# Three PSUM tiles in place of one for the spread of the batch-norm parameters

## The chip, the cores and the metric

The kernel runs on one core of a Trainium2 chip. The metric is device time in microseconds (us). All profiles told here were taken in the fast state, with a granted TensorE clock of 1.0. A profile's span (from the first instruction to the last) is 1.7 to 2.0 us shorter than the time of the same execution.

## The reference, cut to what matters

```python
batch, channels, h, w = 32, 128, 32, 32          # x is 16.78 MB of float32
normalized = (x - running_mean) / sqrt(running_var + eps)
out = maximum(normalized * gamma + beta, 0)       # per channel, in inference
```

So out = relu(x * scale + bias), with one scale and one bias for each channel. The chip has to read 16.78 MB and write 16.78 MB and does little else.

## The kernel before

A row of 1024 values belongs to one channel. 16 rows lie on each of 128 partitions, in two halves of 8 MB each (t = 0 and 1). Loads go out on the queue of SP, parameters and stores on that of ACT.

```python
TILES = ((0, 0, 2), (0, 2, 4), (0, 4, 8), (0, 8, 16), (1, 0, 16))
LOAD_CUTS = {(1, 8)}        # the last tile is loaded in two transfers
STORE_CUTS = {(0, 1)}       # the first tile is stored in two
...
raw = params.tile([Q, 4, J], F32, name="raw")
for k, src in enumerate((running_var, gamma, running_mean, beta)):
    nc.scalar.dma_start(out=raw[:, k, :], in_=src.rearrange("(q j) -> q j", j=J))
...
cols = psum.tile([P, 4, J], F32, name="cols")
for a, b in ((0, 2), (2, 3), (3, 4)):             # three matmuls into one PSUM tile
    nc.tensor.matmul(cols[:, a:b, :] ..., rep ..., raw[:, a:b, :] ..., start=True, stop=True)
nc.scalar.activation(out=std_t, in_=cols[:, 0, :], func=ACTF.Sqrt, bias=eps_t[:, 0:1], scale=1.0)
nc.vector.reciprocal(out=rstd_t, in_=std_t)
nc.vector.tensor_mul(out=scale_t, in0=cols[:, 1, :], in1=rstd_t)
nc.vector.tensor_mul(out=ms_t, in0=cols[:, 2, :], in1=scale_t)
nc.vector.tensor_sub(out=bias_t, in0=cols[:, 3, :], in1=ms_t)
# then on ACT, in order: relu(scale * x + bias) row by row in place, and a store after each tile
...
```

Every transfer of x moves one unbroken piece for each of the 128 partitions, eight pieces for each of the 16 DMA engines. The packet records of the trace show one packet for a piece: loads of 8, 8, 16, 32, 32 and 32 KB, stores of 4, 4, 8, 16, 32 and 64 KB. The records give queue, start, duration and size, but not the engine. What is said here of single engines comes from chaining: a packet starts within a few ns of the end of the one before it on its engine. With work on both queues the packets of a chain nearly always alternate, one load and one store, whatever their size (702 of 720 successions in the changed kernel; chains may be crossed where two packets end together). I call one load packet on each of the 16 engines a *load turn*. The 32 KB loads make 24 load turns.

Of the kernel before, what the change touches and what calls it, by code (L numbers as in the profile page):

```python
# [1 line left out]

# [4 lines left out]


F32 = mybir.dt.float32
ACTF = mybir.ActivationFunctionType  # L10



J = 16

TILES = ((0, 0, 2), (0, 2, 4), (0, 4, 8), (0, 8, 16), (1, 0, 16))

LOAD_CUTS = {(1, 8)}
STORE_CUTS = {(0, 1)}

HALVES = {(1, 0), (1, 1)}


@with_exitstack
def kernel(
    ctx: ExitStack,
    tc: tile.TileContext,
    x: bass.AP,
    gamma: bass.AP,
    beta: bass.AP,  # L30
    running_mean: bass.AP,
    running_var: bass.AP,
    eps: bass.AP,
    out: bass.AP,
):
    nc = tc.nc
    B, C, H, W = x.shape
    HW = H * W
    P = nc.NUM_PARTITIONS
    assert C % J == 0 and P % (C // J) == 0 and (B * C) % (P * J) == 0  # L40
    Q = C // J
    T = B * C // (P * J)

    xr = x.rearrange("b c h w -> (b c) (h w)").rearrange("(t p j) w -> t p j w", p=P, j=J)
    outr = out.rearrange("b c h w -> (b c) (h w)").rearrange("(t p j) w -> t p j w", p=P, j=J)

    data = ctx.enter_context(tc.tile_pool(name="data", bufs=1))
    params = ctx.enter_context(tc.tile_pool(name="params", bufs=1))
    psum = ctx.enter_context(tc.tile_pool(name="psum", bufs=1, space=bass.MemoryType.PSUM))

    tiles = []
    for t, a, b in TILES:
        xt = data.tile([P, b - a, HW], F32, name=f"x{t}_{a}")
        cuts = [a] + [j for j in range(a + 1, b) if (t, j) in LOAD_CUTS] + [b]
        for c, d in zip(cuts, cuts[1:]):
            nc.sync.dma_start(out=xt[:, c - a : d - a, :], in_=xr[t, :, c:d, :])  # L56
        tiles.append((t, a, b, xt))



    raw = params.tile([Q, 4, J], F32, name="raw")
    for k, src in enumerate((running_var, gamma, running_mean, beta)):
        nc.scalar.dma_start(out=raw[:, k, :], in_=src.rearrange("(q j) -> q j", j=J))
    eps_t = params.tile([P, 1], F32, name="eps_t")
    nc.vector.memset(eps_t, float(eps))  # L65
    rep = params.tile([Q, P // Q, Q], F32, name="rep")
    nc.gpsimd.memset(rep, 1.0)  # L67
    nc.gpsimd.affine_select(  # L68
        out=rep,
        in_=rep,  # L70
        compare_op=mybir.AluOpType.is_equal,
        fill=0.0,
        base=0,
        pattern=[[0, P // Q], [-1, Q]],
        channel_multiplier=1,
    )
    cols = psum.tile([P, 4, J], F32, name="cols")


    for a, b in ((0, 2), (2, 3), (3, 4)):  # L80
        nc.tensor.matmul(  # L81
            cols[:, a:b, :].rearrange("p k j -> p (k j)"),
            rep.rearrange("q r s -> q (r s)"),
            raw[:, a:b, :].rearrange("q k j -> q (k j)"),
            start=True,
            stop=True,
        )
    std_t = params.tile([P, J], F32, name="std_t")
    nc.scalar.activation(out=std_t, in_=cols[:, 0, :], func=ACTF.Sqrt, bias=eps_t[:, 0:1], scale=1.0)  # L89
    rstd_t = params.tile([P, J], F32, name="rstd_t")  # L90
    nc.vector.reciprocal(out=rstd_t, in_=std_t)  # L91
    scale_t = params.tile([P, J], F32, name="scale_t")
    nc.vector.tensor_mul(out=scale_t, in0=cols[:, 1, :], in1=rstd_t)  # L93
    ms_t = params.tile([P, J], F32, name="ms_t")
    nc.vector.tensor_mul(out=ms_t, in0=cols[:, 2, :], in1=scale_t)  # L95
    bias_t = params.tile([P, J], F32, name="bias_t")
    nc.vector.tensor_sub(out=bias_t, in0=cols[:, 3, :], in1=ms_t)  # L97

    with tc.manual_schedule(engines={mybir.EngineType.Activation}):
        for t, a, b, xt in tiles:  # L100
            first = a
            for j in range(a, b):
                step = HW // 2 if (t, j) in HALVES else HW
                for w in range(0, HW, step):
                    nc.scalar.activation(  # L105
                        out=xt[:, j - a, w : w + step],
                        in_=xt[:, j - a, w : w + step],
                        func=ACTF.Relu,
                        bias=bias_t[:, j : j + 1],
                        scale=scale_t[:, j : j + 1],  # L110
                    )
                if j + 1 == b or (t, j + 1) in STORE_CUTS:
                    nc.scalar.dma_start(
                        out=outr[t, :, first : j + 1, :], in_=xt[:, first - a : j + 1 - a, :]
                    )
                    first = j + 1


# [1 line left out]
_INS = ['x', 'gamma', 'beta', 'running_mean', 'running_var', 'eps']  # L120
_OUTS = [((32, 128, 32, 32), 'float32')]

_NUMBERS = {'eps': 1e-05}


# [26 lines left out]
```

## Time and profile before

| | kernel before |
|---|---|
| time, median of 3 | 83.53 us (83.52 to 83.58) |
| span of the profile | 81.7 us |
| loads (q1), share of 16 engines' span | 48.6%, or 39.7 us |
| stores (q10) | 47.8%, or 39.1 us |
| ACT busy | 39.1 us |
| last x load landed, last store issued | 46.74 us, 55.95 us |

A share in the queue table is the time that the packets of a queue took, over the time of 16 engines. Multiplied by the span it gives microseconds in which all 16 engines work for that queue.

The prediction doesn't show the chain of waits as lines. Here are its two longest pieces before (start, length, what):

```profile
8.11 38.63 DMA x<-in_x_dram
...
47.91 8.01 ACT x L105 x7
```

The last load of x, issued at 8.11, lands 38.63 us later, and the last activations follow.

### The profile page before, as it was taken

The page shows a single profiled execution, that of the slowest core. Times are in us where ns is not written, and L with a number is a line of the kernel's source. Part 1 is how long each engine was busy: PE and PEld are TensorE (multiplying, and loading weights), DVE is VectorE, ACT ScalarE, POOL GpSimd, SP SyncE. Part 2 cuts the span into 40 slices and gives each one's busy share as a digit, 9 for nine tenths or more (in the row PEclk, how much of TensorE's full clock was granted, in tenths as well). Part 3 has the DMA queues.
Part 4 walks back from the last instruction along what each step waited for, and adds up shares of the span by engine and source line. Part 5 has one row for each costly group of instructions (what it writes and reads, how often), then busy time and mean ns, then how long its engine had stood idle before and what let it go on. Part 6 is the DMA issues. An engine that isn't in the chain of part 4 may idle for free.

```text
span 81.7 us, 128 instructions
## 1 busy us (share of the span) xinstructions
PE 1.7 (2%) x6; PEld 1.5 (2%) x6; DVE 0.8 (1%) x5; ACT 39.1 (48%) x36; POOL 0.8 (1%) x6
## 2 busy tenths in 40 slices
PE   0008000000000000000000000000000000000000
PEld 0007000000000000000000000000000000000000
DVE  0000300000000000000000000000000000000000
ACT  0600477799039999199997199993000000000000
POOL 3000000000000000000000000000000000000000
DMA  2899999989899898969789699996991999998290
GB/s 44 313 422 481 409 481 417 497 369 497 369 385 481 375 491 357 541 293 605 321 373 589 273 489 393 513 497 273 513 770 64 449 513 513 513 513 385 128 513 0
DMA packets 1793, 33.56 MB, mean 411 GB/s; under 512 B 257, under 2 KB 257, under 8 KB 513
## 3 DMA queue, kind: packets, MB, share of 16 engines
q1 hardware_dynamic: 864, 16.78, 48.6%
q10 hardware_dynamic: 928, 16.78, 47.8%
q14 instruction: 1, 0.00, 0.0%
HBM read 16.78 MB, written 16.78 MB: 411 GB/s over the span
## 4 chain that ended last, share of the span: by engine, by line
DMA 56%; ACT 10%; issue 2%; SPq 0%
DMA x<-in_x_dram 56%; ACT x L105 10%; SPq L56 0%
## 5 line engine op out<-in xcount | busy, mean ns | idle before, releaser
L105 ACT ACTIVATE x<-x,bias_t,scale_t 128x1024 f32<-128x1024 f32 (+1 forms) x34 | 37.5, 1178 | 10.0 <-DMA x<-in_x_dram 7.7
L89 ACT ACT_TABLE_LOAD x1 | 1.3, 1283 | 2.7 <-issue 2.7
L89 ACT ACTIVATE std_t<-cols,eps_t 128x16 f32<-128x16 f32 x1 | 0.3, 276 | 4.2 <-PE cols L81 4.2
L81 PE MATMUL cols<-raw,rep 8*128 8x16 f32 (+1 forms) x6 | 1.7, 384 | 6.4 <-DMA raw<-in_gamma_dram 6.3
L81 PEld LDWEIGHTS cols<-raw,rep 8*128 8x128 f32 x6 | 1.5, 307 | 6.5 <-issue 6.3
L68 POOL TENSOR_SCALAR_AFFINE_SELECT rep<-rep 8x128 f32<-8x128 f32 x1 | 0.4, 394 | 0.1
L91 DVE RECIPROCAL rstd_t<-std_t 128x16 f32<-128x16 f32 x1 | 0.3, 253 | 7.5 <-ACT std_t L89 7.5
L67 POOL MEMSET rep<- 8x128 f32 x1 | 0.2, 195 | 0.3 <-POOLq L133 0.3
L93 DVE TENSOR_TENSOR scale_t<-cols,rstd_t 128x16 f32<-128x16 f32 x1 | 0.2, 174 | 0.1
L95 DVE TENSOR_TENSOR ms_t<-cols,scale_t 128x16 f32<-128x16 f32 x1 | 0.2, 174 | 0.0
L97 DVE TENSOR_TENSOR bias_t<-cols,ms_t 128x16 f32<-128x16 f32 x1 | 0.2, 174 | 0.0
L133 POOL MEMSET const-bfloat16-1.0<- 128x1 bf16 x1 | 0.1, 108 | 0.0
L133 POOL MEMSET const-float32-0.0<- 128x1 f32 x1 | 0.1, 105 | 0.3 <-issue 0.3
L133 POOL MEMSET const-uint8-127<- 128x1 uint8 x1 | 0.1, 107 | 0.0
L133 POOL MEMSET const-float32-1.0<- 128x1 f32 x1 | 0.1, 105 | 0.0
L65 DVE MEMSET eps_t<- 128x1 f32 x1 | 0.1, 59 | 0.9 <-PEq L133 0.9
## 6 DMA issues: line engine op xcount, KB each, us to landing
x<-in_x_dram SPq DMA_DIRECT2D x3, 4096.0 KB, 38.6
out_dram<-x ACTq DMA_DIRECT2D x1, 4096.0 KB, 28.6
x<-in_x_dram SPq DMA_DIRECT2D x2, 1024.0 KB, 5.8
x<-in_x_dram SPq DMA_DIRECT2D x1, 2048.0 KB, 11.3
out_dram<-x ACTq DMA_DIRECT2D x1, 2048.0 KB
out_dram<-x ACTq DMA_DIRECT2D x2, 512.0 KB, 19.1
out_dram<-x ACTq DMA_DIRECT2D x1, 1024.0 KB
raw<-in_running_var_dram ACTq DMA_DIRECT2D x1, 0.5 KB
```

What stands on the lines that cost most here:

```text
L65: nc.vector.memset(eps_t, float(eps))
L67: nc.gpsimd.memset(rep, 1.0)
L68: nc.gpsimd.affine_select(out=rep, in_=rep, compare_op=mybir.AluOpType.is_equal, fill=0.0, base=0, pattern=[[0, P // Q], [-1, Q]], channel ...
L81: nc.tensor.matmul(cols[:, a:b, :].rearrange("p k j -> p (k j)"), rep.rearrange("q r s -> q (r s)"), raw[:, a:b, :].rearrange("q k j -> q ...
L89: nc.scalar.activation(out=std_t, in_=cols[:, 0, :], func=ACTF.Sqrt, bias=eps_t[:, 0:1], scale=1.0)
L91: nc.vector.reciprocal(out=rstd_t, in_=std_t)
L93: nc.vector.tensor_mul(out=scale_t, in0=cols[:, 1, :], in1=rstd_t)
L95: nc.vector.tensor_mul(out=ms_t, in0=cols[:, 2, :], in1=scale_t)
L97: nc.vector.tensor_sub(out=bias_t, in0=cols[:, 3, :], in1=ms_t)
L105: nc.scalar.activation(out=xt[:, j - a, w : w + step], in_=xt[:, j - a, w : w + step], func=ACTF.Relu, bias=bias_t[:, j : j + 1], scale=sc ...
L133: nc = _bacc.Bacc("TRN2", target_bir_lowering=False, num_devices=1)
```

## The change

The intent: the square root reads only the columns of the first matmul. In one shared tile it waits for all three. With a tile for each matmul it waits for its own, and the activations and stores can start earlier.

```diff
-    raw = params.tile([Q, 4, J], F32, name="raw")
-    for k, src in enumerate((running_var, gamma, running_mean, beta)):
-        nc.scalar.dma_start(out=raw[:, k, :], ...)
+    raw = {}
+    for a, srcs in ((0, (running_var, gamma)), (2, (running_mean,)), (3, (beta,))):
+        raw[a] = params.tile([Q, len(srcs), J], F32, name=f"raw{a}")
+        for k, src in enumerate(srcs):
+            nc.scalar.dma_start(out=raw[a][:, k, :], ...)
...
-    cols = psum.tile([P, 4, J], F32, name="cols")
+    cols = []
     for a, b in ((0, 2), (2, 3), (3, 4)):
+        c = psum.tile([P, b - a, J], F32, name=f"cols{a}")
         nc.tensor.matmul(
-            cols[:, a:b, :]..., rep..., raw[:, a:b, :]...,
+            c..., rep..., raw[a]...,
             start=True, stop=True)
+        cols.append(c)
...   # the square root and the DVE steps read cols[0], cols[1], cols[2]
```

More of the change, by code (lines that the diff above doesn't have):

```diff
@@ L57 @@
         tiles.append((t, a, b, xt))
-    raw = params.tile([Q, 4, J], F32, name="raw")
-    for k, src in enumerate((running_var, gamma, running_mean, beta)):
-        nc.scalar.dma_start(out=raw[:, k, :], in_=src.rearrange("(q j) -> q j", j=J))
+    raw = {}
+    for a, srcs in ((0, (running_var, gamma)), (2, (running_mean,)), (3, (beta,))):
+        raw[a] = params.tile([Q, len(srcs), J], F32, name=f"raw{a}")
+        for k, src in enumerate(srcs):
+            nc.scalar.dma_start(out=raw[a][:, k, :], in_=src.rearrange("(q j) -> q j", j=J))
     eps_t = params.tile([P, 1], F32, name="eps_t")
@@ L76 @@
     )
-    cols = psum.tile([P, 4, J], F32, name="cols")
+    cols = []
     for a, b in ((0, 2), (2, 3), (3, 4)):
+        c = psum.tile([P, b - a, J], F32, name=f"cols{a}")
         nc.tensor.matmul(
-            cols[:, a:b, :].rearrange("p k j -> p (k j)"),
+            c.rearrange("p k j -> p (k j)"),
             rep.rearrange("q r s -> q (r s)"),
-            raw[:, a:b, :].rearrange("q k j -> q (k j)"),
+            raw[a].rearrange("q k j -> q (k j)"),
             start=True,
@@ L87 @@
         )
+        cols.append(c)
     std_t = params.tile([P, J], F32, name="std_t")
-    nc.scalar.activation(out=std_t, in_=cols[:, 0, :], func=ACTF.Sqrt, bias=eps_t[:, 0:1], scale=1.0)
+    nc.scalar.activation(
+        out=std_t, in_=cols[0][:, 0, :], func=ACTF.Sqrt, bias=eps_t[:, 0:1], scale=1.0
+    )
     rstd_t = params.tile([P, J], F32, name="rstd_t")
@@ L92 @@
     scale_t = params.tile([P, J], F32, name="scale_t")
-    nc.vector.tensor_mul(out=scale_t, in0=cols[:, 1, :], in1=rstd_t)
+    nc.vector.tensor_mul(out=scale_t, in0=cols[0][:, 1, :], in1=rstd_t)
     ms_t = params.tile([P, J], F32, name="ms_t")
-    nc.vector.tensor_mul(out=ms_t, in0=cols[:, 2, :], in1=scale_t)
+    nc.vector.tensor_mul(out=ms_t, in0=cols[1][:, 0, :], in1=scale_t)
     bias_t = params.tile([P, J], F32, name="bias_t")
-    nc.vector.tensor_sub(out=bias_t, in0=cols[:, 3, :], in1=ms_t)
+    nc.vector.tensor_sub(out=bias_t, in0=cols[2][:, 0, :], in1=ms_t)
     with tc.manual_schedule(engines={mybir.EngineType.Activation}):
```

## The prediction

> **What bounds the kernel now.** I read four views in this order: the page, the chain of waits, a table of stretches, and the timeline of the start.
>
> The page first, its slices and its DMA queues:
>
> ```profile
> span 81.7 us, 128 instructions
> ...
> ACT  0600477799039999199997199993000000000000
> ...
> DMA  2899999989899898969789699996991999998290
> ...
> q1 hardware_dynamic: 864, 16.78, 48.6%
> q10 hardware_dynamic: 928, 16.78, 47.8%
> ...
> HBM read 16.78 MB, written 16.78 MB: 411 GB/s over the span
> ```
>
> ScalarE (ACT) is done after slice 28 of 40; the DMA engines are busy from the second slice to the last but one. Loads (q1) take 48.6% of the time of 16 engines and stores (q10) 47.8%: 96.4% of 81.7 us, or 78.8 us, in which all 16 are moving bytes. Single slices jump (a packet is counted where its record falls), so I averaged over long stretches. The table of stretches says, with the DMA share in the last column but one:
>
> ```profile
> 2.00:20.00 18.00, 1.75 (x6) 1.49 (x6) 0.78 (x4) 10.80 (x10) 0.00 (x0) 1.00 1.00 419
> 20.00:40.00 20.00, 0.00 (x0) 0.00 (x0) 0.00 (x0) 14.62 (x16) 0.00 (x0) 1.00 1.01 432
> 40.00:60.00 20.00, 0.00 (x0) 0.00 (x0) 0.00 (x0) 13.65 (x12) 0.00 (x0) 1.00 1.03 444
> 60.00:80.00 20.00, 0.00 (x0) 0.00 (x0) 0.00 (x0) 0.00 (x0) 0.00 (x0) 1.00 0.97 421
> ```
>
> From 2 to 80 us the share is 1.00, 1.01, 1.03 and 0.97: there is no hole to fill. That includes the stretch in which the parameters are made. Before 2 us stands the launch and the first load's latency; after 80 us only the last landing and the closing barriers.
>
> The chain of waits of the page (part 4) attributes 56% to the loads of x and 10% to ACT line 105, then stops at the last activation. It leaves out the last store, which is 24.9 us from issue to landing. So the chain is a chain of data, and the load in it is long because the engines share their time with stores; I take the shares of the DMA engines, not this chain, as the bound.
>
> Last, the start, where the change acts:
>
> ```profile
> 6.33 1.78 PE L81 MATMUL cols<-raw,rep 8*128 8x32 f32 x6 [6.33 <-DMA raw<-in_gamma_dram]
> 8.15 0.28 ACT L89 ACTIVATE std_t<-cols,eps_t 128x16 f32<-128x16 f32 x1 [4.21 <-PE cols L81]
> 8.45 0.25 DVE L91 RECIPROCAL rstd_t<-std_t 128x16 f32<-128x16 f32 x1 [7.52 <-ACT std_t L89]
> 8.82 0.17 DVE L93 TENSOR_TENSOR scale_t<-cols,rstd_t 128x16 f32<-128x16 f32 x1
> 9.03 0.17 DVE L95 TENSOR_TENSOR ms_t<-cols,scale_t 128x16 f32<-128x16 f32 x1
> 9.23 0.17 DVE L97 TENSOR_TENSOR bias_t<-cols,ms_t 128x16 f32<-128x16 f32 x1
> 9.44 1.24 ACT L105 ACTIVATE x<-x,bias_t,scale_t 128x1024 f32<-128x1024 f32 x1 [1.02 <-DVE bias_t L97]
> ```
>
> Six TensorE passes (two for each matmul) end at 8.11 and the square root begins at 8.15, straight after the last of them. It needs only the first matmul, whose two passes end at 6.94 (the second starts at 6.54 and takes 0.40). So it waits for two matmuls that it doesn't read.
>
> **What the Trainium skill says.** "DMA: Bandwidth & Descriptors", section "Issuing engines are not separate DMA queues": transfers from SP and ACT run on the same 16 engines and interleave. The trace agrees: q1 and q10 together fill 96.4% of one set of 16. Its "Specifications" give 435 GB/s as the ceiling of the fabric and about 358 GB/s as the HBM limit for a core; the trace has 419 to 444 GB/s in the four stretches, so it is at the first and above the second, and the measurement decides. "PSUM — Partial Sum Buffer", section "PSUM bank collisions raise a hardware error": a TensorE write and a ScalarE or VectorE read of one bank must be kept apart by waits even where the columns differ. That is why one shared tile makes a reader of columns 0 to 15 wait for the writers of columns 32 to 63; with three tiles that wait can go, if they lie in different banks. I have not seen the addresses; the changed kernel builds and passes the race and memory check. "Perfetto Trace Analysis", section "Identifying Dependency Chains": an instruction that waits on several engines may have an extra semaphore instruction before it. The trace agrees: scale_t, the only one of the four DVE steps that waits on two semaphores, starts 0.11 us after the step before it (8.45 + 0.25 to 8.82), the next two only 0.03 after theirs.
>
> **The change part by part.** The comparison of the two instruction orders shows the same instructions on every engine in the same order: four parameter loads, six TensorE passes, one square root, four DVE steps, 34 activations, six stores, six loads of x. No bytes are added and no duration has a reason to change. Only waits move:
>
> 1. *Removed:* the square root's wait for the second and third matmul. It can start at 6.94 + 0.04 = 6.98 in place of 8.15.
> 2. *Unchanged:* the three matmuls wait for the same four parameter loads, and each already waited for its own slice. TensorE starts at 6.33 as before and the third matmul ends at 8.11.
> 3. *Added:* ms_t and bias_t now each wait for a matmul as well as for the DVE step before. From the row of scale_t that costs 0.11 - 0.03 = 0.08 us each.
> 4. *The new short chain:* square root 6.98 to 7.26; reciprocal from 7.28 (same 0.02 distance as now) to 7.53; scale_t 7.64 to 7.81; ms_t 7.92 to 8.09 (second matmul done at 7.48: its second pass starts at 7.11 and takes 0.37); bias_t 8.20 to 8.37, third matmul done at 8.11, so it doesn't bind. The first activation follows at 8.41, where it now starts at 9.44: **1.0 us earlier**. Gain 1.17, less 0.16 for the two added waits.
> 5. *What lies behind it:* the first four activations and three stores move 1.0 us earlier (first store issued about 9.7, now 10.71), and so do the next four (from 15.61 to about 14.6; their 2 MB load lands about 13.0: issued near 1.7, 11.3 to landing). Then ACT reaches a wait that no parameter ends:
>
> ```profile
> 23.84 9.16 ACT L105 ACTIVATE x<-x,bias_t,scale_t 128x1024 f32<-128x1024 f32 x8 [3.59 <-DMA x<-in_x_dram]
> 33.02 0.34 ACTq L113 DMA_DIRECT2D out_dram<-x  x1
> ...
> 46.77 9.16 ACT L105 ACTIVATE x<-x,bias_t,scale_t 128x1024 f32<-128x1024 f32 x8 [2.27 <-DMA x<-in_x_dram]
> 55.95 0.34 ACTq L113 DMA_DIRECT2D out_dram<-x  x1
> ```
>
> The 3.59 us of idle time before 23.84 become about 4.6. The 1.0 us is swallowed there, 24 us into the kernel.
>
> 6. *The sum:* on the DMA engines, 0 packets removed, 0 added, 0 holes closed. The span stays 81.7 and the time 83.5.
>
> **The rivals.**
>
> *A: the 1.0 us comes through.* If the end hung on the chain from the parameters over the activations to the stores, all of it would show: 83.53 - 1.0 = 82.5 us, 1.2%, still under 2%. For it: a store can only start after an activation. Against it: the engines have loads to move in that time, so an earlier store displaces a load, and the last activations wait for loads. I give it 3%.
>
> *B: earlier stores delay the loads and the last store comes too late.* Store packets would take turns with load packets from about 1.0 us sooner. The packet records show a 32 KB load packet at 1.22 us and a 4 KB store packet at 0.16 us, one of each in turn, so 1.0 us is less than one turn (1.38 us): one more store packet of 0.16 to 0.31 us on each engine before the last load lands. Landing 46.74 becomes 46.9 to 47.05, and the issue of the last store 55.95 becomes 56.1 to 56.25. Does that open a hole? The packets of the last store start at 60.90, and those of the store before end at 61.24, without a gap; from the end of its issue (56.29) to its first packet there are 4.6 us. The first store took 3.5 us for the same (11.09 to 14.56), while queued behind loads, so at least 1.1 us of slack remain for a delay of at most 0.3. A hole would cost its own length; at worst a few tenths: 83.8 us. I give it 5%.
>
> *C: the added waits or a late tile eat the gain.* If x's first tile were late, the first activation would not move. It isn't: the first load lands 4.8 us after its issue at 0.81, under 6 us. If the three tiles lay in one bank and waited still, nothing would move at all. Either way the time is 83.5, the same as mine, and only the start of the trace tells it apart.
>
> **Range and chances.** The three runs before lie between 83.52 and 83.58. The engines do 78.8 us of packets plus fixed ends in both kernels; what can differ is how the 16 engines finish (their last packets now end between 80.29 and 80.56, a spread of 0.27) and scatter between chips. So 83.5, with 83.3 to 83.7 to hold it 8 times in 10. Faster by over 2% needs 1.67 us, more than the whole 1.0 us that moves: 1%. Slower by over 2% needs a hole of 1.67 us, against a possible delay of 0.3 and slack of 1.1: 1%. Within 2%: 98%.
>
> **What would show each step right or wrong.** Right: the square root at about 7.0, the first activation at about 8.4, first store issue at about 9.7, idle time before the eight activations near 24 us grown from 3.59 to about 4.6, last store issued between 55.9 and 56.3, DMA share about 1.00 in all four stretches, span 81.6 to 81.8. Step 1 is wrong if the square root still starts after 8.1; step 3 if the gaps before ms_t and bias_t stay at 0.03 or exceed 0.11; step 5 if the eight activations near 24 us move earlier by more than 0.3. The prediction as a whole is wrong if the last store is issued more than 1 us later, if the DMA share falls below 0.95 in a stretch before 80 us, or if packets of the same size take longer than before.

## The result, and the profile after

The changed kernel takes 84.12 us (median of 6, 83.90 to 84.20), the kernel before 83.50 in the same rounds (83.41 to 83.58). The ratio is 1.007, 95% interval 1.0056 to 1.0084. A ratio is the mean time of one kernel's fast runs over that of the other's of the same rounds, so it is not quite the ratio of the medians quoted here. The 0.6 us are clear of the scatter, and 84.12 is outside the range of 83.3 to 83.7. The two traces lie a little further apart than the medians: that of the kernel before is of an execution of 83.44 us, that of the changed kernel of 84.20, the slowest of its six.

The start first, in the timeline of the changed kernel (start, length, engine, line, operation, and in brackets the idle time before it and what ended it):

```profile
6.30 1.76 PE L84 MATMUL cols<-raw,rep 8*128 8x32 f32 x6 [6.30 <-DMA raw<-in_gamma_dram]
6.95 0.27 ACT L93 ACTIVATE std_t<-cols,eps_t 128x16 f32<-128x16 f32 x1 [3.06 <-PE cols L84]
...
7.62 0.17 DVE L99 TENSOR_TENSOR scale_t<-cols,rstd_t 128x16 f32<-128x16 f32 x1
7.89 0.17 DVE L101 TENSOR_TENSOR ms_t<-cols,scale_t 128x16 f32<-128x16 f32 x1
8.17 0.18 DVE L103 TENSOR_TENSOR bias_t<-cols,ms_t 128x16 f32<-128x16 f32 x1
8.39 1.24 ACT L111 ACTIVATE x<-x,bias_t,scale_t 128x1024 f32<-128x1024 f32 x1 [1.17 <-DVE bias_t L103]
```

The intent worked. The square root starts at 6.95 in place of 8.15 and the first activation at 8.39 in place of 9.44.

Later in the same timeline come the points where ACT waits for loads, and the last store:

```profile
24.03 9.16 ACT L111 ACTIVATE x<-x,bias_t,scale_t 128x1024 f32<-128x1024 f32 x8 [4.84 <-DMA x<-in_x_dram]
...
47.85 9.16 ACT L111 ACTIVATE x<-x,bias_t,scale_t 128x1024 f32<-128x1024 f32 x8 [3.19 <-DMA x<-in_x_dram]
57.03 0.34 ACTq L119 DMA_DIRECT2D out_dram<-x  x1
```

At 24 us ACT is already 0.19 us later than before (23.84), and at 47.85 it is 1.08 us later (46.77). The chain of waits gives the reason in one line: the last load takes 39.67 us from issue to landing in place of 38.63.

```profile
8.15 39.67 DMA x<-in_x_dram
```

Now the page, the lines that answer to those of before:

```profile
span 82.5 us, 129 instructions
...
ACT  0601778993039999199996079996000000000000
...
DMA  1999999989898989789789499997991999999190
...
q1 hardware_dynamic: 864, 16.78, 48.8%
q10 hardware_dynamic: 928, 16.78, 47.3%
...
HBM read 16.78 MB, written 16.78 MB: 407 GB/s over the span
```

The queue table is where the loss shows. Loads take 48.8% of 82.5 us, or 40.3 us, in place of 39.7. Stores take 47.3%, or 39.0 us, as before. Packets and bytes are the same. So the same load packets took 0.55 us longer, on the average over the 16 engines, out of a span that grew by 0.8.

The table of stretches has the stretch, its length, the busy time of five engines, the clock, the DMA share and GB/s. For the changed kernel:

```profile
2.00:20.00 18.00, 1.75 (x6) 1.49 (x6) 0.78 (x4) 11.04 (x10) 0.00 (x0) 1.00 1.01 423
20.00:40.00 20.00, 0.00 (x0) 0.00 (x0) 0.00 (x0) 14.22 (x14) 0.00 (x0) 1.00 0.99 424
40.00:60.00 20.00, 0.00 (x0) 0.00 (x0) 0.00 (x0) 13.81 (x13) 0.00 (x0) 1.00 1.02 425
60.00:80.00 20.00, 0.00 (x0) 0.00 (x0) 0.00 (x0) 0.00 (x0) 0.00 (x0) 1.00 1.03 446
```

The share is 1.00 in all stretches here too. It can't tell a slow packet from a fast one: an engine in a slow packet is busy. GB/s can. The stretch 34 to 48 us, in which the last eight load turns run, is first shown for the kernel before, then for the changed one:

```profile
34.00:48.00 14.00, 0.00 (x0) 0.00 (x0) 0.00 (x0) 10.95 (x12) 0.00 (x0) 1.00 1.02 438
```

```profile
34.00:48.00 14.00, 0.00 (x0) 0.00 (x0) 0.00 (x0) 9.87 (x11) 0.00 (x0) 1.00 1.02 415
```

The share is 1.02 in both, but the engines moved 438 GB/s before and 415 after.

The packet records of the trace give the place. All packets of a size take the same time when nothing disturbs them: 309 ns for 8 KB, 611 for 16, 1213 for 32, 2418 for 64. A 4 KB packet takes 159 ns. In both traces no store packet is more than 20 ns above its figure. The 32 KB load packets average 1221 ns before and 1246 after, so 24 of them lose 0.6 us on each engine. Most of that falls in one place: the very last load turn, which starts at 45.0 us in the changed kernel, takes 1.75 to 1.93 us on all 16 engines (mean 1.80). Before, it takes 1.21 to 1.33 (mean 1.245). The first loads of 8 KB are slow in both (0.56 us per engine over 309 ns a packet before, 0.43 after), but the last of them is followed by the first 16 KB packet at the same time in both (7.46 and 7.47 us in the mean), so they don't explain it.

### The profile page after: what moved, and what is told of

It is laid out like the page before. It is cut to its first block, busy times and chain, and to the rows that moved or that the text cites. A ratio compares the mean times of both kernels' runs of the same rounds, so it can differ in the third digit from the quotient of the medians.

```text
span 82.5 us, 129 instructions
## 1 busy us (share of the span) xinstructions
PE 1.7 (2%) x6; PEld 1.5 (2%) x6; DVE 0.8 (1%) x5; ACT 39.1 (47%) x36; POOL 0.8 (1%) x6
## 3 DMA queue, kind: packets, MB, share of 16 engines
q1 hardware_dynamic: 864, 16.78, 48.8%
q10 hardware_dynamic: 928, 16.78, 47.3%
## 4 chain that ended last, share of the span: by engine, by line
DMA 56%; ACT 10%; issue 2%; SPq 0%
DMA x<-in_x_dram 56%; ACT x L111 10%; SPq L56 0%
## 6 DMA issues: line engine op xcount, KB each, us to landing
x<-in_x_dram SPq DMA_DIRECT2D x3, 4096.0 KB, 39.7
```

## The experiments

The theory after the result: **turns**. The first store is issued 1.06 us earlier, so the first store packet of an engine comes after one 32 KB load packet in place of two. In that alignment (the order in which load and store packets stand beside each other) loads are slowed by the stores beside them, most of all the last load turn. Rivals: the tiles themselves cost something (addresses, added waits); the slow packets fall at random; the late loads and the stores beside them clash in memory by their addresses; the load queue runs empty behind the last turn.

This table sums up the traces. "Loads, us" is the q1 share times the span, from each page. The next three columns are counted in the packet records: how many 32 KB load packets an engine has moved before its first store packet, the mean of all 384 such load packets, and the mean of the last 16 of them. A packet or turn that is so many ns *over* took that much longer than an undisturbed packet of its size. Times are medians, but a trace is of one execution: those of the changed kernel (84.20 us) and of a_late_first (83.98) are of their slowest.

| run | first store issued, us | load packets ahead | loads, us | 32 KB load, mean ns | its last turn, mean ns | time, us | ratio |
|---|---|---|---|---|---|---|---|
| before | 10.71 | 2 | 39.7 | 1221 | 1245 | 83.53 | 1 |
| b_again | 10.59 | 2 | 39.8 | 1226 | 1213 | 83.63 | 1.0017 |
| changed | 9.65 | 1 | 40.3 | 1246 | 1803 | 84.12 | 1.0070 |
| a_again | 9.57 | 1 | 40.3 | 1246 | 1588 | 84.14 | 1.0073 |
| p_psum_only | 9.55 | 1 | 40.3 | 1247 | 1629 | 84.17 | 1.0065 |
| a_delay05 | 10.15 | 2, on two engines 1 | 39.8 | 1227 | 1366 | 84.07 | 1.0073 |
| a_delay10 | 10.84 | 2 | 39.8 | 1223 | 1213 | 83.62 | 1.0010 |
| a_late_first | 11.53 | mostly 3 | 40.1 | 1238 | 1311 | 83.72 | 1.0027 |
| a_delay20 | 12.18 | 3 | 40.1 | 1236 | 1519 | 84.02 | 1.0054 |
| a_delay33 | 13.30 | mostly 4 | 40.3 | 1247 | 1612 | 84.27 | 1.0084 |
| b_late_stores | 32.6 | 20 | 40.5 | 1256 | 1791 | 84.37 | 1.0110 |
| a_late_stores | 32.6 | 20 | 40.4 | 1250 | 1911 | 84.29 | 1.0094 |

### Both kernels again

No edit.

> The kernel before, unchanged, for a second trace of it. All theories: ratio 1.000 within 0.002, about 83.5 us. If slow load packets are what costs the changed kernel its time (in its trace the 32 KB load packets took 1246 ns in the mean against 1221 before, with one turn of all 16 engines at about 1.8 us near 45 us), this trace must again show a mean near 1220 ns and no such turn. If slow turns fall at random, this trace may show one too.

> The changed kernel, unchanged, for a second trace of it. Ratio 1.006 to 1.008. Timing theory (earlier stores put load and store packets in another alignment, and loads are slowed by that): slow load packets at the same place again, a turn of about 1.8 us near 45 us on all engines. Chance theory: slow packets elsewhere or none, and then the 0.6 us must be visible somewhere else.

Measured: 83.63 and 84.14 us, ratios 1.0017 (1.0004 to 1.003) and 1.0073 (1.006 to 1.0086). The second trace of the kernel before has no slow last turn (all 16 packets at 1213 ns); the second trace of the changed one has it again, 1588 ns in the mean. So the slow turn isn't chance. The first run also says how far a ratio may stray with the same code: 0.0017. Differences below about 0.003 are not read in what follows.

### One part of the change alone: the PSUM tiles

```diff
 # of the change, only this part; the four parameters stay in one raw tile
-    cols = psum.tile([P, 4, J], F32, name="cols")
+    cols = []   # one PSUM tile for each matmul, appended in the loop
```

> One part of the change alone: three PSUM tiles, but the four parameters stay in one raw tile. The matmuls already waited each for its own part of the raw tile, so the early start must come from the PSUM tiles alone: square root at about 7.0, first store issued at about 9.65, and the whole loss: 1.006 to 1.008. If the raw tiles carried part of the loss, less: 1.000 to 1.004.

Measured: 84.17 us, 1.0065 (1.0037 to 1.0094), the first store issued at 9.55 us. The PSUM tiles carry all of the early start and the loss. The raw tiles do nothing that shows.

### The early start undone, the tiles kept

```diff
-    for a, b in ((0, 2), (2, 3), (3, 4)):
+    for a, b in ((2, 3), (3, 4), (0, 2)):      # a_late_first
```

> Three PSUM tiles and three raw tiles kept, but the matmul that the square root needs is issued last, so that the early start is undone: square root at about 8.1 us, first activation at about 9.4. Timing theory: the loss goes, ratio 0.998 to 1.002. Theory that the tiles themselves cost (addresses, banks, more waits): the loss stays, 1.006 to 1.008.

```diff
+    junk = params.tile([P, 930], F32, name="junk")                     # a_delay10
+    nc.gpsimd.memset(junk, 0.0)
     with tc.manual_schedule(engines={mybir.EngineType.Activation}):
+        nc.scalar.activation(out=junk, in_=junk, func=ACTF.Relu,
+                             bias=bias_t[:, 0:1], scale=scale_t[:, 0:1])
```

> The changed kernel with one activation on a scratch tile of 128x930 ahead of the first activation on x, which takes about 1.05 us of ACT: first activation on x back at about 9.4 us with the whole of the change kept. Timing theory: ratio 0.998 to 1.002. Tile theory: 1.006 to 1.008, and if ACT time counted at all, up to 1.02.

The delay did what was meant. ACT does 1.16 us of useless work, the first store goes out at 10.84 us, and the loss is gone: 83.62 us, ratio 1.0010 (0.9997 to 1.0023). The page and the stretch from 34 to 48 us of this run:

```profile
span 81.9 us, 131 instructions
...
q1 hardware_dynamic: 864, 16.78, 48.6%
```

```profile
34.00:48.00 14.00, 0.00 (x0) 0.00 (x0) 0.00 (x0) 10.78 (x11) 0.00 (x0) 1.00 1.02 434
```

48.6% of 81.9 is 39.8 us for the loads, and GB/s is back at 434. All parts of the change are in this kernel; only the moment at which its activations and stores start is back (and a scratch tile is added). So the moment is the cause, not the tiles. That it is the stores' moment, and not the activations', is shown by the runs with held stores below.

The other run was a miss of mine. TensorE ran its matmuls in the order written and now waited for running_mean first, until 7.32 us. The square root started at 8.96, and the first store went out at 11.53, 0.8 us later than before in place of at the same time. The time was 83.72 with a wide spread (83.44 to 83.98), ratio 1.0027 (1.0009 to 1.0045). It is no clean undoing, but one more point on the scale of delays.

### The scale of delays

The same edit with other sizes: one scratch activation of 300 columns, two of 930, three of 900.

> The changed kernel with a scratch activation of 128x300 ahead of the first on x: first store issued about 0.5 us later than in the changed kernel, 0.5 us earlier than before. Theory of turns (the loss depends on how many load packets of the 32 KB loads each DMA engine has moved when its first store packet comes: one in the changed kernel, two before): either one load packet, with the loss whole (84.1) and a slow last load turn near 45 us, or two, with no loss (83.5); nothing between. Theory that each tenth of a us of earlier store costs something: about half the loss, 83.8.

> The changed kernel with two scratch activations of 128x930: first store issued about 2.3 us later than in the changed kernel, near 12.0 us, so three load packets ahead of the first store packet, as in the run with the matmul issued last. Theory of turns: the same time as that run, 83.6 to 83.8, with the slow last load turn absent or below 150 ns. Theory that only earlier than before is bad: 83.5.

> The changed kernel with three scratch activations of 128x900: first store issued about 3.4 us later than in the changed kernel, near 13.0 us, so four load packets ahead of the first store packet. Theory of turns: no general trend with the delay, a value of its own between 83.4 and 84.1. If the delay of ACT itself mattered, the time would grow by the 2.4 us beyond before: 85.9. If the engines are the bound, under 84.1.

Measured: 84.07, 84.02 and 84.27 us (ratios 1.0073, 1.0054 and 1.0084). So there is no trend. Stores 0.6 us earlier than before lose 0.5 us, and stores 1.5 or 2.6 us later lose 0.4 to 0.7. The kernel before stood on a good point of this scale, and the change moved it off. That an early start is bad in itself fell with the last two runs, and so did my guess that a delay of three packets would keep its last turn below 150 ns over (it was 306). The times of both, too, were above the ranges that the theory of turns had given them (83.6 to 83.8, and 83.4 to 84.1).

A part of these losses isn't the packets'. The time exceeds the span by 1.71 us in the mean of the runs of the changed kernel and of the kernel before, but by 1.79 to 1.81 with one scratch activation, by 1.91 with two (a_delay20) and 1.88 with three (a_delay33). So about 0.2 us of the last two losses lie outside the span; what they are is not known.

The half-way run is the most telling one. I had expected all or nothing. Its packet records show 14 engines with two 8 KB store packets left after their last load packet, as before, and two engines with one, as in the changed kernel. On the 14 that last load packet took 1.21 to 1.39 us. On the two it took 1.86 and 1.99 us; they started it last, at 45.0 us, the others from 44.5 to 44.9. Those two engines ended at 81.04 and 81.14 us, the 14 at 80.58 or earlier. So within one run the slow packets belong to the engines in the other alignment, and two late engines are enough for the loss, since the kernel ends with its last engine. Two other traces have a single engine out of step. In a_swap (below) 15 engines have the alignment of the changed kernel and the last load packet takes them 1.67 to 1.89 us; the one with that of the kernel before takes 1.213 us and is done at 80.24 us, the others from 80.81. In b_j32 it is the reverse: 15 engines at 1.213 us, and 1.549 on the one with the alignment of the changed kernel. An engine out of step also starts its last load packet first or last, so alignment and moment can't be told apart there.

The half-way run also shows why the mean over the engines (39.8 us of loads, as before) can hide it. The number of packets left isn't the whole rule, though: in the run with the matmul issued last, two engines had two left, and their last load packets took 1.24 and 1.47 us, no less than those of the engines with three (1.21 to 1.40).

### What about the last load turn is it?

```diff
-TILES = ((0, 0, 2), (0, 2, 4), (0, 4, 8), (0, 8, 16), (1, 0, 16))   # a_swap; cuts exchanged too
+TILES = ((1, 0, 2), (1, 2, 4), (1, 4, 8), (1, 8, 16), (0, 0, 16))
+    tail = data.tile([P, 128], F32, name="tail")                       # a_extra_load, after the loads
+    nc.sync.dma_start(out=tail, in_=xr[1, :, 15, 0:128])
-STORE_CUTS = {(0, 1)}
+STORE_CUTS = {(0, 1), (0, 3)}                                          # a_split_store
-LOAD_CUTS = {(1, 8)}
+LOAD_CUTS = {(1, 8), (1, 12)}                                          # a_cut12
```

Each is an edit of the changed kernel by itself.

> The changed kernel with the two 8 MB halves of the batch exchanged: the same packets in the same order and turns, but the first tiles are loaded from and stored to the second half and the last load comes from the first half. Theory of turns (it is the order of packets on a DMA engine that counts): ratio 1.006 to 1.008, a slow last turn of the 32 KB loads again, 350 to 600 ns per engine over 1213. Theory that the addresses of the late loads and of the stores beside them clash in memory: another value, 1.000 to 1.004, slow turns elsewhere or none.

> The changed kernel with one more small load (512 B on each of 128 partitions, unused) queued behind the last load of x. If the last 32 KB load turn is slow because the load queue runs empty behind it, the turn becomes normal (under 100 ns over 1213) and the ratio 1.000 to 1.003, or the delay moves to the small packets. If it is slow because of which store packets stand beside it, it stays: 350 to 600 ns, ratio 1.006 to 1.008.

> The changed kernel with the store of the second tile cut in two, so that the last loads stand beside 4 KB store packets in place of 8 KB ones, in the same turns, with the same store start. If the end of a store transfer beside the end of the load transfer makes the slow turn: still slow (350 to 600 ns), ratio 1.005 to 1.008. If the size or the addresses of the 8 KB packets make it: 1.000 to 1.003.

> The changed kernel with the last load of x cut in two of 16 KB packets: more turns, so the last eight load turns stand beside 16 KB store packets. If any last load turn of this early start is slow: a slow last 16 KB turn, 350 to 600 ns over 611, ratio 1.005 to 1.008. If it is the pair of 32 KB loads and 8 KB stores: no slow turn at the end, ratio 0.998 to 1.003.

Measured:

| run | time, us | ratio | last 32 KB load turn, mean ns | other slow turns |
|---|---|---|---|---|
| a_swap | 84.11 | 1.0086 | 1754 | none above 70 ns over |
| a_extra_load | 84.59 | 1.0131 | 1659 | one of 203 over, at 34 us |
| a_split_store | 84.54 | 1.0138 | 1838 | the one before it, 256 over |
| a_cut12 | 84.41 | 1.0114 | 1535, at 33 us | two 16 KB turns at 41 and 42 us, 119 and 105 over |

- The halves of memory don't matter: with them exchanged the slow turn stays. The exchange moves the addresses by 8 MB and leaves their lower digits as they were, so a clash that hangs on these is not excluded.
- The queue that runs empty doesn't matter: with another load behind it the turn stays. The 64 KB added cost 8 packets of 27 ns, 0.22 us on each engine; another 0.15 us or so lie outside the span (time less span is 1.87 us in the mean, against 1.71); the rest of the 0.5 us that this run is slower than the changed kernel is not explained.
- The size of the store packets beside it doesn't matter: with 4 KB packets it stays, and the turn before it becomes slow too.
- With the last load in 16 KB packets, the end of the loads isn't slow any more. What is slow is the last packet of 32 KB, at 33 us, and the turns at 41 and 42 us. The loss isn't smaller, though 0.2 us of it lie outside the span (1.90 us).

The times of the last three runs are above every range that I had given them; of a_cut12 both expected outcomes failed.

So the loss moves with the packets, but I found no single pair of transfers that makes it.

### Are shared turns needed?

```diff
+HOLD = (1, 3)
-                    nc.scalar.dma_start(out=outr[t, :, first : j + 1, :], in_=...)
+                    held.append((outr[t, :, first : j + 1, :], ...))
                     first = j + 1
+                if (t, j) >= HOLD:
+                    for dst, src in held:
+                        nc.scalar.dma_start(out=dst, in_=src)
+                    held = []
```

> The kernel before with the first five stores held back until the fourth activation of the last tile, about 38 us, so that the loads run nearly alone and the stores follow. Theory that turns of loads and stores slow the loads: load turns at 1213 ns almost throughout, time at or a little below before, ratio 0.995 to 1.000. If mixing loads and stores is what keeps the engines full, slower: above 1.01.

> The changed kernel with the same hold. The first activation is again 1.0 us earlier than in the kernel before, but no store starts earlier. Theory of turns: the same time as the kernel before with the hold, within 0.002, the loss of 0.007 gone. If the change costs by itself, 0.006 to 0.008 above it.

Measured: 84.37 us for the kernel before with the hold, 84.29 for the changed one (ratios 1.0110 and 1.0094 to the kernel before without it). The expected time of both was a miss: the hold itself costs 0.9 us. The hold was also shorter than meant: the stores were issued from 32.6 us on, not at 38. What the pair was for held: with no store started earlier, the changed kernel isn't slower, though its first activation again starts 1.2 us sooner (8.36 to 9.52). The stretches of the changed kernel with the hold say where its loss is:

```profile
12.00:34.00 22.00, 0.00 (x0) 0.00 (x0) 0.00 (x0) 16.27 (x16) 0.00 (x0) 1.00 1.01 434
34.00:44.00 10.00, 0.00 (x0) 0.00 (x0) 0.00 (x0) 8.48 (x10) 0.00 (x0) 1.00 0.98 379
44.00:48.00 4.00, 0.00 (x0) 0.00 (x0) 0.00 (x0) 4.00 (x4) 0.00 (x0) 1.00 1.06 449
```

From 12 to 34 us loads run alone at 434 GB/s. The first 19 of the 24 load turns, the last of which starts at 34.1 us, are at most 1 ns above 1213 in their means. The first store packets come at 36.4 us; from there to the end of the loads GB/s falls, and the last load turn takes 1911 ns. After the loads, stores alone run at 449. So from 12 us on loads alone are at full rate and stores alone are at full rate. Nearly all of the loss lies where they share the engines.

I then tried to hold the stores until the loads were over.

```diff
-HOLD = (1, 3)
+HOLD = (1, 6)      # a_hold6; (1, 7) in a_hold7
```

> The changed kernel with the first five stores held until the seventh column of the last tile: issue near 36 us, first store packet near 40 us, so one or two load turns are shared. Theory that shared turns slow the loads, most of all the last: the last turn still slow, 84.0 to 84.4, or, if it takes several shared turns, 83.3 to 83.6.

> The same held until the eighth column: issue near 37 us, first store packet near 41 us, at about the end of the loads (41.3 us). Theory that shared turns slow the loads: all load turns at 1213 ns, excess of the 32 KB loads under 100 ns per engine, and 83.2 to 83.4 if the engines find store packets without a hole; every 0.1 us of hole adds 0.1. If the last load turn is slow here too, sharing is not the reason and the loss belongs to the change from loads to stores itself.

Measured: 84.38 and 84.40 us. These two runs failed as experiments. The stores went out at 32.6 us in both, as with the shorter hold: the instruction that issues a store waits only for its own tile, long done, and didn't wait for the activations written ahead of it. They are two more repeats of the run before them, with last load turns of 1831 and 1707 ns. A kernel whose stores never share a turn with loads has not been run.

### Another split of the batch

```diff
-J = 16
+J = 32
-TILES = (..., (0, 8, 16), (1, 0, 16))
+TILES = (..., (0, 8, 16), (0, 16, 32))     # 32 rows on a partition; the cuts moved with it
```

> The kernel before with 32 rows of the batch on a partition in place of 2 times 16: the same sizes, packets and turns, but a row pitch of 128 KB in place of 64 KB, so other addresses beside each other. Theory of turns alone: 83.5 as before, ratio 0.998 to 1.003. Theory of addresses: a value of its own.

> The changed kernel with 32 rows on a partition. Theory of turns alone: slower than the kernel before with 32 rows by 0.006 to 0.008, with a slow last load turn of 350 to 600 ns. Theory of addresses: the loss differs, or is gone.

Measured: 83.64 us for the kernel before, 84.04 for the changed one (ratios 1.0027 and 1.0068 to the kernel before with 16 rows). With other addresses the change still loses, but 0.4 us in place of 0.6, and the last load turn is hardly slow (1303 ns). The loss is spread over it and turns at 34 and 44 us (141 and 168 ns over). The alignments are those of the pair with 16 rows (two load packets ahead of the first store on 15 of 16 engines, then one). So the loss goes with the alignment in both. That the layout in memory has a part in which turns pay it is not shown: it is one trace, and the second trace of the changed kernel has slow turns at 34 and 44 us too (102 and 96 ns over). The range I gave for this pair (0.006 to 0.008) was too high and the slow turn of 350 to 600 ns wasn't there.

## Why the prediction was wrong

By its own steps:

- **Bound.** Right. The DMA engines are the bound in both kernels; between 2.5 and 79 us the packet records leave each engine idle for less than 0.01 us.
- **Steps 1 to 5 up to the first wait for a load.** Right. (That it is the sharing of one PSUM bank which makes the reader wait is not shown: no run gives the addresses. p_psum_only shows that three PSUM tiles end the wait.) Square root 6.98 predicted, 6.95 measured; first activation 8.41 and 8.39; added waits 0.08 us each (the gaps before ms_t and bias_t are 0.10 and 0.11, from 0.03); first store about 9.7 and 9.65; idle time near 24 us about 4.6 and 4.84.
- **"No bytes are added and no duration has a reason to change", and from it step 6, the sum of 0.** This failed. The 32 KB load packets went from 1221 to 1246 ns in the mean, 24 on each engine: 0.6 us. The page agrees, with 0.55 us more for the loads. I had named "packets of the same size take longer than before" as what would make the prediction wrong, but gave it no weight, because I read the DMA share of 1.00 as proof that nothing could change in those stretches. Another of its signs came true, the last store issued more than 1 us later (57.03 in place of 55.95); the third, a share below 0.95, did not.
- **Rival B.** It was right that earlier stores delay the loads, and wrong in size. It allowed 0.16 to 0.31 us; the last load landed 1.08 us later. One more 8 KB store packet per engine (0.31) is in it, as B had it. The longer load packets (0.6) were missing, and the remaining 0.2 is about the size of what the engines drifted apart: their last packets end within 0.34 us of each other before and 0.50 after (the prediction read 0.27 for the 0.34: the first engine ends at 80.21, not at 80.29). B's hole never opened. The last store was issued 1.08 us later and its packets still followed those of the store before. The loss came by slower packets, not by waiting.
- **Rivals A and C.** Neither happened. C's bound of 83.5 rested on the same failed step.
- **Range.** 0.2 us on either side covered the scatter of one kernel, 0.17 in the runs before. It left out that another alignment of the same packets could move the time: the delayed runs show 0.1 to 0.7 us, of which up to 0.2 lie outside the span.

What stays open is why two load packets ahead of the first store are the good alignment (all engines or all but one have it in the four traces without a slow last turn: before, b_again, a_delay10 and b_j32), and what inside the engines or the memory makes the last 32 KB load packet 0.1 to 0.7 us longer in the others. The runs exclude the tiles, the half of memory, the empty queue and the size of the store packets beside it. They don't name the mechanism. No version here beats the kernel before; the changed kernel with a delay of 1 us only equals it.

## What to carry to other kernels

A DMA share of 1.00 says that the engines are busy, not that they are fast. Multiply each queue's share by the span, and compare GB/s in the same stretch, before you call a DMA-bound time fixed. When a kernel is bound by DMA and loads share the engines with stores, moving the start of a store by half a microsecond can cost or give back half a microsecond with not one byte changed, so expect that much scatter between variants, and test it by a delay that does nothing else. Look at single engines too: two late ones out of 16 set the end.

## What the Trainium skill lacked or had wrong

- "DMA: Bandwidth & Descriptors", section "Issuing engines are not separate DMA queues", says that transfers from several queues run on the same engines and interleave. It lacks that a packet can take longer where loads and stores share the engines: 32 KB load packets took 1213 ns alone and 1.75 to 1.93 us in the last shared turn of the changed kernel.
- The same page, "Queues, rings and completion order", has each engine take turns between queues at packets. The traces agree, with one partition's piece of a transfer for each turn. It doesn't say what follows for the shares: with 4 KB store packets beside 32 KB load packets the stores get 0.16 of 1.38 us.
- The same page, "Specifications", gives about 358 GB/s as the limit of HBM for a core. The runs moved 406 to 411 GB/s over the whole span and 434 with loads alone. The row is not wrong but lacks its condition, which the page's section "Bandwidth" has: the limit is a core's share when both cores of a pair are streaming. This kernel runs on one core.
- The same table gives a first-byte latency of about 0.6 us. The first load of x agrees: 0.64 us from the end of its issue (1.18) to its first packet (1.82). What the table lacks is the wait on busy engines: with loads queued, the first store waited 3.3 us from the end of its issue (10.02) to its first packet (13.34), 3.5 before.
- "Perfetto Trace Analysis", "Identifying Dependency Chains", says that a wait on several engines may bring an extra semaphore instruction. The traces agree (one before scale_t in the kernel before, and also before ms_t and bias_t in the changed one), and the page has no price for it: on DVE it was 0.07 to 0.08 us.
